# The Newton steps of the dilated heads' norms, on POOL instead of DVE, in a two-layer hybrid decoder trunk

## The chip, the cores and the metric

The kernel runs on one core of one Trainium2 chip. A core has five engines with a queue each: PE (TensorE, matrix products), DVE (VectorE) and ACT (ScalarE) for elementwise work, POOL (GpSimd), and SP, which only issues transfers here. Each engine works through its own row of instructions in order; where one needs what another engine makes, it waits on a semaphore and everything behind it in its row waits too. The metric is device time in microseconds (us) of one execution.

## The reference

Two layers over 256 tokens of width 1024. Each layer normalizes x, projects it by one wide matrix, and feeds three mixers: a causal convolution with 31 taps, a block-sparse attention with 8 heads ("NSA"), and three dilated banded attentions with 4 heads each. The change touches only the norm of the heads of the dilated queries and keys:

```python
def rms_norm(x, g):
    xf = x.astype(jnp.float32)
    y = xf * lax.rsqrt(jnp.mean(xf * xf, axis=-1, keepdims=True) + NORM_EPS)
    return (y * g.astype(jnp.float32)).astype(x.dtype)

def dilated_mixer(q, k, v, pos, qn, kn):
    ...
    for gi, (w, r) in enumerate(DIL_PAIRS):
        qh = rope(rms_norm(split_heads(qs[gi], DIL_HEADS), qn), pos)
        kh = rope(rms_norm(split_heads(kss[gi], DIL_HEADS), kn), pos)
        ...
        o, lse = banded_attention(phase(qh)[:, :, None], phase(kh), phase(vh), w // r, Q_BLOCK)
    ...

for l in range(DEPTH):
    h = rms_norm(x, attn_norm[l])
    (...) = jnp.split(h @ w_in[l], splits, axis=-1)
    x = x + jnp.concatenate([y_a, y_b, y_c], axis=-1) @ w_out[l]
    x = x + conv_ffn(rms_norm(x, ffn_norm[l]), w_up[l], ffn_dw[l], ffn_dw_b[l], w_down[l])
```

## The kernel before, in words

Tokens lie on the 128 partitions in two tiles. A product in full precision is made of three: the weights are split into `whi` (a rounded copy, made by ACT, line 210) and `wlo` (the rest, made by DVE, line 213), the activations in the same way, and PE adds three matmuls (lines 452 to 454). The weights stream in from memory in pieces of up to 128x1024 (`raw`); every piece passes ACT and DVE before PE can use it. `Dq`, `Dk`, `Dv` are the projections of the dilated queries, keys and values, `oa` and `ob` the output projection, `up` and `da`/`db` the feed-forward part.

`rope` (line 549 on) makes a normalized and rotated head tile. For each token tile DVE multiplies the projection by a cosine and a sine table into `z1` and `z2` and adds them; ACT squares the heads one at a time (line 568) and leaves the sums in `a` (`radq` or `radk`). Then the reciprocal root `r` of all heads at once (12 columns for the dilated heads) comes from a bit trick and three Newton steps: 12 small DVE instructions, each needing the one before it. At last DVE multiplies `z1` by `r` (`z1dq<-z1dq,rrdq`), PE transposes the result (`tpdq`, `tpdk`, line 880), and ACT copies it to `dq` or `dk`, from which the scores are made.

`dil_qk` calls `rope` four times in a layer: queries and keys (`dq`, `dk`), for each of two halves of the heads (0 and 1). With two layers that is eight chains of Newton steps. They stand in the mixer part of a layer, among the NSA pairs, the convolution's taps (`acc<-a_pad,dwh,acc`, 60 in a layer on DVE) and the splitting of weights. The string `ORDER` gives the order in which the program is written; a scheduler with a cost model of its own then sets each engine's row, so that an instruction that changes engine also moves others.

Of the kernel before, what the change touches and what calls it, by code (L numbers as in the profile page):

```python
# [14 lines left out]
I32 = mybir.dt.int32  # L15
AF = mybir.ActivationFunctionType
ALU = mybir.AluOpType
# [10 lines left out]
EPS = 1e-6  # L28
BIG = 1e30
TAPS = 31  # L30
MAGIC = float(0x5F3759DF)
# [157 lines left out]
def tile_hybrid_trunk(ctx, tc, x_in, pos_in, stream, feats, gains, norms, const_in, out):  # L189
    nc = tc.nc  # L190
# [21 lines left out]
    def tt(o, a, b, op):  # L212
        return nc.vector.tensor_tensor(out=o, in0=a, in1=b, op=op)  # L213

    def ts(o, a, s1, s2, op0, op1=None, eng=None):
        e = eng or nc.vector
        if op1 is None:
            e.tensor_scalar(out=o, in0=a, scalar1=s1, scalar2=None, op0=op0)
        else:
            e.tensor_scalar(out=o, in0=a, scalar1=s1, scalar2=s2, op0=op0, op1=op1)  # L220

    def stt(o, a, s, b, op0, op1):
        return nc.vector.scalar_tensor_tensor(out=o, in0=a, scalar=s, in1=b, op0=op0, op1=op1)  # L223
# [172 lines left out]
    def pool_tt(o, a, b, op):  # L396
        nc.gpsimd.tensor_tensor(out=o, in0=a, in1=b, op=op)
# [106 lines left out]
    for l in range(L):  # L504
# [45 lines left out]
        def rope(srcs, H, q, slots, nm, dup=False, np_=P):  # L550
            n = len(srcs)

            def small(tag):
                return mp.tile([P, n * H], F32, tag=tag, name=f"{tag}{nm}", bufs=2)[:np_]

            a, r, h_, t_ = (small(x) for x in ("ra", "rr", "rh", "rt"))
            z1s = []
            for i in range(n):
                v = srcs[i].rearrange("p (h d) -> p h d", h=H)
                z1 = mp.tile([P, H * 64], F32, tag="zr", name=f"z1{nm}{i}", bufs=ZB)[:np_].rearrange("p (h d) -> p h d", h=H)  # L560
                z2 = mp.tile([P, H, 64], F32, tag="z2", name=f"z2{nm}{i}", bufs=1)[:np_]
                cb = ctab[q][:np_, slots[i]].rearrange("p a b -> p (a b)").unsqueeze(1).broadcast_to([np_, H, 64])
                tt(z1, v, cb, ALU.mult)
                sb = stab[q][:np_, slots[i]].unsqueeze(1).broadcast_to([np_, H, 2, 32])
                tt(z2.rearrange("p h (a b) -> p h a b", a=2), v.rearrange("p h (a b) -> p h a b", a=2)[:, :, ::-1, :], sb, ALU.mult)
                sq = mp.tile([P, 64], F32, tag="sq", name=f"sq{nm}{i}", bufs=2)[:np_]
                for h in range(H):
                    nc.scalar.activation(out=sq, in_=v[:, h], func=AF.Square, accum_out=a[:, i * H + h:i * H + h + 1])  # L568
                tt(z1, z1, z2, ALU.add)
                z1s.append(z1)  # L570
            ts(a, a, 1.0 / 64.0, EPS, ALU.mult, ALU.add)
            ts(r.bitcast(I32), a.bitcast(I32), -0.5, MAGIC, ALU.mult, ALU.add)
            ts(h_, a, -0.5, None, ALU.mult)
            for _ in range(3):
                tt(t_, r, r, ALU.mult)
                tt(t_, t_, h_, ALU.mult)
                stt(r, t_, 1.5, r, ALU.add, ALU.mult)
            outs = []
            for i in range(n):
                rv = r[:, i * H:(i + 1) * H].unsqueeze(2)  # L580
                if dup:
                    d = mp.tile([P, H * 2 * 64], F32, tag="zr", name=f"zd{nm}{i}", bufs=ZB)[:np_]
                    tt(d.rearrange("p (h u d) -> p h u d", h=H, u=2), z1s[i].unsqueeze(2).broadcast_to([np_, H, 2, 64]),
                       rv.unsqueeze(3).broadcast_to([np_, H, 2, 64]), ALU.mult)
                    outs.append(d)
                else:
                    tt(z1s[i], z1s[i], rv.broadcast_to([np_, H, 64]), ALU.mult)
                    outs.append(z1s[i].rearrange("p h d -> p (h d)"))
            return outs
# [25 lines left out]
        def section_a(split):  # L615
            banks = tok_chunk("a", 512, split, f"A{l}")
            if split:
                late_loads()
            kss = []
            ksw = mp.tile([P, 3, 256], F32, tag="dk", name="ksw", bufs=1)  # L620
            for t in range(NT):
                bk = banks[t].rearrange("p (a e) -> p a e", a=2)
                ks = ksw[:, t]
                copy_act(ks.rearrange("p (a e) -> p a e", a=2), bk[:, :, 0:P])
                copy_act(vN[:, t], bk[:, :, P:2 * P])
                kss.append(ks)
            krs = rope(kss, 4, 1, (0, 1), "k", dup=True)
            for t in range(NT):
                kr = krs[t]
                tp = tp_bank(f"tpk{t}")  # L630
                for i in range(4):
                    nc.tensor.transpose(tp[:, i * P:(i + 1) * P], kr[:, i * P:(i + 1) * P], ident)
                tv = tp.rearrange("p (w g c) -> p w g c", w=2, g=2)
                split_keys(slice(P - t * P, 2 * P - t * P), tv[:, 0])
                split_keys(slice(272 + t * P, 272 + t * P + P), tv[:, 1])

        def section_a0(split):
# [43 lines left out]
            for g in range(2):  # L681
                nc.tensor.matmul(cp2[0:64, 64 + g * 64:128 + g * 64], hv[64:P, g].rearrange("p r c -> p (r c)"), w2[64:P], start=True, stop=True)
            kcd = rope([cp2[0:32, 0:64]], 1, 1, (2,), "c", dup=True, np_=32)[0]
            for g in range(2):
                tt(vbig[:, g], cp2[0:64, 64 + g * 64:128 + g * 64].unsqueeze(1).broadcast_to([64, 4, 64]),
# [13 lines left out]
        QS = mp.tile([P, 8, S], F32R, tag="QT", name="QS", bufs=1)  # L699
        banks = tok_chunk("b", 512, False, f"B{l}")  # L700
        qrs = rope(banks, 8, 0, (0, 1), "q")
        for t in range(NT):
            z = qrs[t].rearrange("p (h d) -> p h d", h=8)
# [167 lines left out]
        def dil_qk(nm, jp):  # L871
            q = 2 if nm == "q" else 3
            dst = mp.tile([P, 3, S], F32, tag=f"d{nm}", name=f"d{nm}{jp}", bufs=1)
            dil_state[nm] = dst
            banks = tok_chunk(f"d{nm}{jp}", 384, False, f"D{nm}{jp}{l}")
            zrs = rope([b[:, 0:384] for b in banks], 6, q, (0, 1), f"d{nm}{jp}")
            for t in range(NT):
                tp = tp_bank(f"tpd{nm}{jp}{t}")
                for i in range(3):
                    nc.tensor.transpose(tp[:, i * P:(i + 1) * P], zrs[t][:, i * P:(i + 1) * P], ident)  # L880
                copy_act(dst[:, :, t * P:(t + 1) * P], tp[:, 0:384].rearrange("p (k c) -> p k c", k=3))
# [80 lines left out]
        for step in ORDER.split():  # L962
            nm, arg = step[:-1].split("(")
            arg = int(arg) if arg.isdigit() else arg.split(",")
            if nm == "dq":
                dil_qk("q", arg)
            elif nm == "dk":
                dil_qk("k", arg)
            else:
                dict(np=nsa_pair, t=conv_taps, nf=nsa_finish, dv=dil_v, da=dil_attn, ds=dil_scores, pv=dil_pv, ct=lambda _: conv_tail())[nm](arg)  # L970

# [127 lines left out]
```

## Time and profile before

| | us |
|---|---|
| median of 3 runs | 751.72 (746.33 to 754.43) |
| the profiled execution, whole | 746.86 |
| its span, first to last instruction | 745.1 |
| PE busy in the span | 718.1 |
| DVE busy | 602.4 |
| ACT busy | 490.5 |
| POOL busy | 26.1 |

The span is 1.8 us shorter than the execution it belongs to. A share of busy time is a mean over stages. One layer takes from about 20 to 372 us, the other from there to the end; in each the mixers come first and the feed-forward part after them. Matmuls overlap in their records, so what PE really does per matmul is read from start to start. The same holds for DVE: its records overlap their neighbours by some 0.08 us.

### The profile page before, as it was taken

How to read it: one execution, taken by the hardware profiler on the slowest of the kernel's cores; microseconds unless marked ns; L12 is line 12 of the kernel's file. 1: busy time of each engine (PE TensorE's matmuls, PEld its weight loads, DVE VectorE, ACT ScalarE, POOL GpSimd, SP SyncE). 2: the span in 40 equal slices, each digit the busy share in tenths (PEclk: the TensorE clock that was granted, in tenths of full speed). 3: DMA queues.
4: the chain of work that ended last, by engine and by line, in shares of the span. 5: the costliest groups of instructions: out<-in, count | busy, mean ns of one | idle time of the engine just before them, and what ended most of it. 6: DMA issues, size and time to landing. Idle time of an engine off the chain costs nothing.

```text
span 745.1 us, 13477 instructions
## 1 busy us (share of the span) xinstructions
PE 718.1 (96%) x4818; PEld 635.4 (85%) x4818; DVE 602.4 (81%) x1393; ACT 490.5 (66%) x1174; POOL 26.1 (4%) x67
## 2 busy tenths in 40 slices
PE   6999989999999999999999998999999999999997
PEld 4789877887899999988877886779789999999885
DVE  7899999987898989944587699999878989988441
ACT  5867998756677667643356589986556767676330
POOL 6300000000000000000040000000000000000000
PEclk9999999999999999999999999999999999999999
DMA  8755123444466565665366231336344665666631
GB/s 312 254 154 149 46 72 114 142 166 160 132 224 209 180 205 185 197 206 196 115 225 211 78 109 40 93 86 187 111 142 170 203 200 193 200 197 197 198 115 56
DMA packets 36005, 119.77 MB, mean 161 GB/s; under 512 B 4113, under 2 KB 4385, under 8 KB 35938
## 3 DMA queue, kind: packets, MB, share of 16 engines
q1 hardware_dynamic: 35714, 118.63, 50.3%
q8 instruction: 38, 0.62, 0.3%
q0 software_dynamic: 224, 0.28, 0.2%
q14 instruction: 29, 0.24, 0.1%
HBM read 117.85 MB, written 1.05 MB: 160 GB/s over the span
## 4 chain that ended last, share of the span: by engine, by line
PE 80%; ACT 9%; DVE 7%; DMA 2%; issue 2%; POOL 0%; SPq 0%; DVEq 0%; ACTq 0%
PE up L454 10%; PE up L452 10%; PE up L453 10%; PE da L454 3%; PE da L452 3%; PE da L453 3%; PE db L452 3%; PE db L454 2%; PE db L453 2%; DVE wlo L213 2%; ACT whi L210 2%; ACT sqq L568 1%; PE o L827 1%; PE Dk L452 1%; PE Dk L453 1%
## 5 line engine op out<-in xcount | busy, mean ns | idle before, releaser
L213 DVE TENSOR_TENSOR wlo<-raw,whi 128x1024 fp32r<-128x1024 f32 (+3 forms) x232 | 259.4, 1125 | 79.8 <-ACT whi L210 79.1
L210 ACT ACTIVATE whi<-raw 128x1024 fp32r<-128x1024 f32 (+3 forms) x232 | 224.5, 980 | 97.6 <-PE db L454 53.6
L452 PE MATMUL up<-xT_hi,whi 128*128 128x256 f32 x640 | 176.8, 276 | 0.0
L453 PE MATMUL up<-xT_lo,whi 128*128 128x256 f32 x640 | 176.7, 276 | 0.0
L454 PE MATMUL up<-xT_hi,wlo 128*128 128x256 f32 x640 | 176.6, 276 | 0.0
L453 PEld LDWEIGHTS up<-xT_lo,whi 128*128 128x128 f32 x640 | 120.1, 188 | 0.0
L452 PEld LDWEIGHTS up<-xT_hi,whi 128*128 128x128 f32 x640 | 120.1, 188 | 0.0
L454 PEld LDWEIGHTS up<-xT_hi,wlo 128*128 128x128 f32 x640 | 120.1, 188 | 0.0
L223 DVE SCALAR_TENSOR_TENSOR u<-up,ffeat,u 128x255 f32<-128x255 f32 (+1 forms) x176 | 79.9, 477 | 2.6
L223 DVE SCALAR_TENSOR_TENSOR acc<-a_pad,dwh,acc 128x256 f32<-128x256 f32 x120 | 54.5, 477 | 0.2
L1052 ACT ACTIVATE sl<-u 128x256 f32<-128x256 f32 x44 | 18.1, 416 | 49.4 <-DVE u L223 49.4
L1045 ACT ACTIVATE u<-up,ffeat 128x256 f32<-128x256 f32 x88 | 44.2, 553 | 0.0
L453 PE MATMUL da<-wlo,gT_hi 128*128 128x512 f32 x88 | 34.3, 389 | 0.0
L452 PE MATMUL da<-whi,gT_hi 128*128 128x512 f32 x88 | 34.3, 389 | 0.0
L454 PE MATMUL db<-whi,gT_lo 128*128 128x512 f32 x88 | 34.2, 389 | 0.0
L454 PE MATMUL da<-whi,gT_lo 128*128 128x512 f32 x88 | 34.2, 389 | 0.0
L452 PE MATMUL db<-whi,gT_hi 128*128 128x512 f32 x88 | 34.2, 389 | 0.0
L453 PE MATMUL db<-wlo,gT_hi 128*128 128x512 f32 x88 | 34.2, 389 | 0.0
L452 PE MATMUL Dv<-whi,xT_hi 128*128 128x384 f32 x64 | 21.9, 347 | 2.7 <-ACT whi L210 2.0
L210 ACT ACTIVATE ms<-ms,dd 128x128 f32<-128x128 f32 (+1 forms) x64 | 24.3, 451 | 0.0
L452 PE MATMUL A<-whi,xT_hi 128*128 128x280 f32 (+1 forms) x64 | 22.9, 358 | 0.3 <-ACT xT_hi L210 0.2
L452 PE MATMUL Dq<-whi,xT_hi 128*128 128x384 f32 x64 | 22.7, 354 | 0.2
(358 smaller groups left out, 1601.4 us busy)
## 6 DMA issues: line engine op xcount, KB each, us to landing
raw<-in_stream SPq DMA_DIRECT2D x172, 512.0 KB, 4.2
raw<-in_stream SPq DMA_DIRECT2D x48, 384.0 KB, 3.3
raw<-in_stream SPq DMA_DIRECT2D x8, 280.0 KB, 4.7
w<-in_stream SPq DMA_DIRECT2D x4, 512.0 KB, 5.7
gain<-in_norms SPq DMA_DIRECT2D x3, 512.0 KB, 3.6
x<-in_x SPq DMA_DIRECT2D x4, 256.0 KB, 4.1
out<-x SPq DMA_DIRECT2D x4, 256.0 KB, 2.0
feat<-in_feats SPq DMA_DIRECT2D x2, 339.0 KB, 4.6
```

The lines of the kernel that those rows point to most:

```text
L210: return nc.scalar.activation(out=o, in_=i, func=AF.Copy, **kw)
L213: return nc.vector.tensor_tensor(out=o, in0=a, in1=b, op=op)
L223: return nc.vector.scalar_tensor_tensor(out=o, in0=a, scalar=s, in1=b, op0=op0, op1=op1)
L452: nc.tensor.matmul(o, a_hi, b_hi, start=start, stop=False)
L453: nc.tensor.matmul(o, a_hi, b_lo, start=False, stop=False)
L454: nc.tensor.matmul(o, a_lo, b_hi, start=False, stop=stop)
L568: nc.scalar.activation(out=sq, in_=v[:, h], func=AF.Square, accum_out=a[:, i * H + h:i * H + h + 1])
L827: nc.tensor.matmul(ob[j * 64:j * 64 + 64, 0:S], vv[0], pTs[pr][j][:, w, 0:2, :].rearrange("p a c -> p (a c)"), start=(w == 0), stop=False, ...
L1045: nc.scalar.activation(out=u[:, h], in_=z, func=AF.Identity, scale=c[:, 2:3], bias=c[:, 3:4])
L1052: nc.scalar.activation(out=sl_, in_=u[:, 0], func=AF.Silu)
```

## The change

For the chains whose name begins with "d" (dilated queries and keys) the Newton steps are issued to POOL. [...] The heads of the NSA mixer keep theirs on DVE.

```diff
-            ts(a, a, 1.0 / 64.0, EPS, ALU.mult, ALU.add)
-            ts(r.bitcast(I32), a.bitcast(I32), -0.5, MAGIC, ALU.mult, ALU.add)
-            ts(h_, a, -0.5, None, ALU.mult)
-            for _ in range(3):
-                tt(t_, r, r, ALU.mult)
-                tt(t_, t_, h_, ALU.mult)
-                stt(r, t_, 1.5, r, ALU.add, ALU.mult)
+            if nm[0] == "d":
+                pool = nc.gpsimd
+                ts(a, a, 1.0 / 64.0, EPS, ALU.mult, ALU.add, eng=pool)
+                ts(r.bitcast(I32), a.bitcast(I32), -0.5, MAGIC, ALU.mult, ALU.add, eng=pool)
+                ts(h_, a, -0.5, 1.0, ALU.mult, ALU.mult, eng=pool)
+                for _ in range(3):
+                    pool_tt(t_, r, r, ALU.mult)
+                    pool_tt(t_, t_, h_, ALU.mult)
+                    ts(t_, t_, 1.5, 1.0, ALU.add, ALU.mult, eng=pool)
+                    pool_tt(r, t_, r, ALU.mult)
+            else:
...
```

The scheduler also gives the rows of DVE, PE and ACT another order. SP's row of transfers stays as it was. Three places show it. The first is DVE at the first query chain (half 0, layer 1), from the row behind the tap that follows the last score reduction; `mn` and `cs` belong to the NSA mixer, `dd` and `ms` to its softmax. Before:

```order
L220 TENSOR_SCALAR radq_1020<-radq_1020 128x12
L806 TENSOR_REDUCE mn_1281<-cs_874 128x8
L220 TENSOR_SCALAR rrdq_1021<-radq_1020 128x12
L218 TENSOR_SCALAR rhdq_1022<-radq_1020 128x12
L213 TENSOR_TENSOR cs_874<-cs_874,mn_1281 128x128
L213 TENSOR_TENSOR rtdq_1023<-rrdq_1021 128x12
L223 SCALAR_TENSOR_TENSOR acc<-a_pad,dwh,acc 128x256
L213 TENSOR_TENSOR rtdq_1023<-rtdq_1023,rhdq_1022 128x12
```

and now, from the same row on:

```order
L817 TENSOR_REDUCE mn_1287<-cs_874 128x8
L223 SCALAR_TENSOR_TENSOR acc<-a_pad,dwh,acc 128x256
L213 TENSOR_TENSOR cs_874<-cs_874,mn_1287 128x128
L223 SCALAR_TENSOR_TENSOR acc<-a_pad,dwh,acc 128x256 x2
L213 TENSOR_TENSOR z1dq_1024<-z1dq_1024,rrdq_1021 128x384
L213 TENSOR_TENSOR z1dq_1036<-z1dq_1036,rrdq_1021 128x384
L792 RECIPROCAL dd_1082<-dd_1082 128x8
L765 ISA ms_1329,negm_1327<-sc_1332,cst 128x128
L765 ISA negm_1327 128x1
L213 TENSOR_TENSOR dd_1082<-dd_1082,sg 128x8
L213 TENSOR_TENSOR wlo_1193<-raw_1190,whi_1192 128x768
L213 TENSOR_TENSOR wlo_1211<-raw_1208,whi_1210 128x768
```

From there 27 rows stood ahead of the multiply by `r` before, both `wlo` pieces among them; now it is five instructions, and the two pieces stand behind it. The second place is POOL's row, where the chain stands alone (`pool_tt` is line 397; `rt` is the Newton scratch, `rh` minus half the mean square); it begins so and goes on with two more steps:

```order
L542 TENSOR_TENSOR stab_348<-sin_t,gsc_204 128x128
L220 TENSOR_SCALAR radq_1020<-radq_1020 128x12
L220 TENSOR_SCALAR rrdq_1021<-radq_1020 128x12
L220 TENSOR_SCALAR rhdq_1022<-radq_1020 128x12
L397 TENSOR_TENSOR rtdq_1023<-rrdq_1021 128x12
L397 TENSOR_TENSOR rtdq_1023<-rtdq_1023,rhdq_1022 128x12
L220 TENSOR_SCALAR rtdq_1023<-rtdq_1023 128x12
L397 TENSOR_TENSOR rrdq_1021<-rtdq_1023,rrdq_1021 128x12
```

Ahead of it stands only the making of the tables at the start of the layer, and nothing but the other chains behind it until the next layer's tables. The third place is PE at the second query chain (half 1, layer 1). Before:

```order
L454 MATMUL Dv_0_2035<-whi_1828,xT_lo 128x384
L452 MATMUL Dv_0_2035<-whi_1846,xT_hi 128x384
L880 MATMUL tpdq_1785<-ident,z1dq_1747 128x128 x3
L880 MATMUL tpdq_1790<-ident,z1dq_1759 128x128 x3
L453 MATMUL Dv_0_2035<-wlo_1847,xT_hi 128x384
```

and now:

```order
L454 MATMUL Dk_0_1815<-whi_1733,xT_lo 128x384
L452 MATMUL Dk_1_1816<-whi_1733,xT_hi 128x384
L891 MATMUL tpdq_1794<-ident,z1dq_1753 128x128 x3
L891 MATMUL tpdq_1799<-ident,z1dq_1765 128x128 x3
L453 MATMUL Dk_1_1816<-wlo_1734,xT_hi 128x384
```

The six transposes stood among the value projection's matmuls and now stand among the key projection's, ahead of the rest of it. Counted by the matmuls of lines 452 to 454 that stand ahead of them in PE's row, the transposes of the eight chains moved up from 354 to 338, 378 to 370, 487 to 463 and 547 to 528 in layer 1, and from 2248 to 2238, 2287 to 2268, 2371 to 2359 and 2434 to 2424 in layer 2: 118 matmuls in all, 19 of them (those of the second key chain of layer 1) the 512 wide ones of the output projection and the others 384 wide.

## Rows read from the trace of the kernel before

**Rows 1.** The page's first part: busy us, share of the span, instructions.

```profile
PE 718.1 (96%) x4818; PEld 635.4 (85%) x4818; DVE 602.4 (81%) x1393; ACT 490.5 (66%) x1174; POOL 26.1 (4%) x67
```

**Rows 2.** Busy us by stretch: PE, PEld, DVE, ACT, POOL; then clock, DMA share, GB/s.

```profile
60.00:190.00 130.00, 126.55 (x796) 105.69 (x796) 116.73 (x369) 98.91 (x311) 0.00 (x0) 1.00 0.37 118
205.00:372.00 167.00, 167.00 (x1212) 156.72 (x1211) 129.15 (x206) 100.94 (x152) 0.00 (x0) 1.00 0.61 191
440.00:570.00 130.00, 124.87 (x792) 103.19 (x791) 114.67 (x355) 98.32 (x303) 0.00 (x0) 1.00 0.34 106
```

**Rows 3.** The same from last square to multiply, eight chains: first, last, sum.

```profile
86.06:91.57 5.51, 5.03 (x37) 4.00 (x36) 5.39 (x27) 5.51 (x18) 0.00 (x0) 1.00 0.04 6
...
516.43:523.58 7.15, 7.15 (x39) 6.57 (x37) 6.70 (x18) 4.66 (x7) 0.00 (x0) 1.00 0.93 315
sum 44.66, PE 41.91 PEld 37.44 DVE 42.81 ACT 32.13 POOL 0.00; mean PE 5.24 PEld 4.68 DVE 5.35 ACT 4.02 POOL 0.00
```

**Rows 4.** Timeline of ACT: the last square of the first query chain.

```profile
85.86 0.20 ACT L568 ACTIVATION_READ_ACCUMULATOR sqdq<-Dq 128x1 f32 x1
```

**Rows 5.** Timeline of DVE, first query chain: start, duration, instruction.

```profile
86.24 0.17 DVE L220 TENSOR_SCALAR radq<-radq 128x12 f32<-128x12 f32 x1
86.32 0.28 DVE L806 TENSOR_REDUCE mn<-cs 128x8 f32<-128x128 f32 x1
...
86.94 0.48 DVE L223 SCALAR_TENSOR_TENSOR acc<-a_pad,dwh,acc 128x256 f32<-128x256 f32 x1
87.34 0.16 DVE L213 TENSOR_TENSOR rtdq<-rtdq,rhdq 128x12 f32<-128x12 f32 x1
...
91.57 1.02 DVE L213 TENSOR_TENSOR z1dq<-z1dq,rrdq 128x384 f32<-128x384 f32 x2
```

**Rows 6.** Timeline of PE: second query chain, then the output projection.

```profile
140.73 0.33 PE L453 MATMUL Dk<-wlo,xT_hi 128*128 128x384 f32 x1
140.91 0.33 PE L454 MATMUL Dk<-whi,xT_lo 128*128 128x384 f32 x1
...
144.92 0.99 PE L880 MATMUL tpdq<-ident,z1dq 128*128 128x128 f32 x6
...
158.04 0.39 PE L453 MATMUL oa<-wlo,yT_hi 128*128 128x512 f32 x1
158.27 0.39 PE L454 MATMUL oa<-whi,yT_lo 128*128 128x512 f32 x1
```

**Rows 7.** Timeline of POOL: a norm's root and Newton steps, one column.

```profile
8.91 0.26 POOL L220 TENSOR_SCALAR naa<-ssa 128x1 f32<-128x1 f32 x1 [4.17 <-ACT junk L335]
9.26 0.18 POOL L220 TENSOR_SCALAR naa<-naa 128x1 f32<-128x1 f32 x1
9.53 0.57 POOL L220 TENSOR_SCALAR nra<-naa 128x1 int32<-128x1 int32 x1
...
10.45 0.34 POOL L220 TENSOR_SCALAR nwta<-nra,nwha 128x1 f32<-128x1 f32 x1
10.90 0.27 POOL L220 TENSOR_SCALAR nra<-nwta,nra 128x1 f32<-128x1 f32 x1
...
13.30 2.81 POOL L220 TENSOR_SCALAR gsc<-grow 128x64 f32<-128x64 f32 x12
```

**Rows 8.** Timeline of DVE and POOL around 30 us: both with SBUF inputs.

```profile
27.15 1.22 DVE L213 TENSOR_TENSOR wlo<-raw,whi 128x1024 fp32r<-128x1024 f32 x1
29.67 0.59 POOL L542 TENSOR_TENSOR ctab<-cos_t,gsc 128x192 f32<-128x192 f32 x1
29.76 1.59 DVE L213 TENSOR_TENSOR wlo<-raw,whi 128x1024 fp32r<-128x1024 f32 x1 [1.39 <-ACT whi L210]
31.27 1.48 DVE L213 TENSOR_TENSOR wlo<-raw,whi 128x1024 fp32r<-128x1024 f32 x1
31.63 1.43 POOL L542 TENSOR_TENSOR ctab<-cos_t,gsc 128x128 f32<-128x128 f32 x1
33.03 0.45 POOL L542 TENSOR_TENSOR stab<-sin_t,gsc 128x128 f32<-128x128 f32 x1
```

More of the change, by code (lines that the diff above doesn't have):

```diff
@@ L570, in rope @@
                 z1s.append(z1)
-            ts(a, a, 1.0 / 64.0, EPS, ALU.mult, ALU.add)
-            ts(r.bitcast(I32), a.bitcast(I32), -0.5, MAGIC, ALU.mult, ALU.add)
-            ts(h_, a, -0.5, None, ALU.mult)
-            for _ in range(3):
-                tt(t_, r, r, ALU.mult)
-                tt(t_, t_, h_, ALU.mult)
-                stt(r, t_, 1.5, r, ALU.add, ALU.mult)
+            if nm[0] == "d":
[9 more added lines that the diff above has]
+            else:
+                ts(a, a, 1.0 / 64.0, EPS, ALU.mult, ALU.add)
+                ts(r.bitcast(I32), a.bitcast(I32), -0.5, MAGIC, ALU.mult, ALU.add)
+                ts(h_, a, -0.5, None, ALU.mult)
+                for _ in range(3):
+                    tt(t_, r, r, ALU.mult)
+                    tt(t_, t_, h_, ALU.mult)
+                    stt(r, t_, 1.5, r, ALU.add, ALU.mult)
             outs = []
```

## The prediction

> **What bounds the kernel now.** The first part of the page comes first: PE is busy for 718.1 of 745.1 us and DVE for 602.4, POOL for 26.1 [rows 1]. Those are means, so the next view is the busy time by stretch [rows 2]. In the feed-forward part PE is busy for all of 167.00 us. In the mixer parts PE is busy for 126.55 and 124.87 of 130 us and DVE for 116.73 and 114.67: PE idles 3.45 and 5.13 us there, DVE 13.3 and 15.3. The granted clock is 1.00 throughout, the upper of the two levels (2.4 GHz). The third view cuts out the eight stretches that the change is about, from the end of a chain's last square on ACT to the start of the multiply by `r` on DVE [rows 3]. The first runs from 86.06 us [rows 4] to 91.57 [rows 5]. Together they last 44.66 us, a mean of 5.58, and in them DVE is busy for 42.81 us and PE for 41.91. So in just these places both are full. The reader is to see that a chain of 12 small operations takes 5.58 us not because DVE is slow at it, but because other work stands between its steps: a step costs DVE 0.08 us from start to start (86.24 to 86.32), a tap 0.40 (86.94 to 87.34) [rows 5]. The chain is slow, and it costs next to nothing.
>
> **What DVE gets back.** Twelve instructions by 0.08 us are 0.96 us a chain, 7.7 us in eight chains. This is all that the change can give DVE, whose 28.6 us of idle time in the mixers say that not all of it would reach the end.
>
> **What the chain costs on POOL.** No row shows POOL at 128x12. The nearest one-input rows are a norm's steps at one column [rows 7]: from start to start 0.35 (8.91 to 9.26), 0.27 (9.26 to the next start at 9.53) and, with two scalars per partition, 0.45 us (10.45 to 10.90). All ten instructions of that norm took from 8.91 to 13.30, 0.44 each. The nearest two-input row is 0.45 us at 128 columns, with 0.59 at 192 [rows 8]: 0.0022 us a column, so about 0.19 at 12 columns, an estimate, plus the 0.09 that lie between the end of one dependent step and the start of the next (9.26 + 0.18 to 9.53) [rows 7]. That is 0.28. I take 0.35 a step, the middle of 0.27 to 0.45, since the steps are of both kinds and each depends on the last: 15 x 0.35 = 5.25 us. The bounds are 15 x 0.28 = 4.2 and 15 x 0.45 = 6.75.
>
> The Trainium skill ("GPSIMD Engine Reference", section 4.1) puts two-input elementwise work on POOL at about twice DVE's time and one-input work at about the same rate. By that rule, from the 0.16 us of such an operation on DVE [rows 5], nine two-input steps and six others would take 9 x 0.32 + 6 x 0.16 = 3.8 us in place of 5.25, and the whole change would cost some 12 us less than the sum below. The rows here have POOL at 0.27 to 0.45 us for a column, so I stay with them.
>
> **What the two engines cost each other.** Alone a `wlo` of 1024 columns takes 1.22 us; beside POOL's products two of them took 1.59 and 1.48, and a POOL product that takes 0.45 alone took 1.43 [rows 8]. So where DVE reads two inputs from SBUF, one waits for the other and they take turns: each turn costs DVE 0.26 to 0.37 us. Taps and `wlo` pieces are such instructions. I take four turns a chain, for the few DVE instructions that stand beside its start (next part), of 0.3 us: 1.2 us. The bounds are none and twice that.
>
> **Where the wait goes.** The multiply by `r` now waits for POOL, and in DVE's row it has moved up. At the first query chain a reduction, a subtraction and three taps lie between the last square and the multiply, 0.2 + 0.2 + 3 x 0.4 = 1.6 us. Read in the same way from the new row with the durations of before, the other seven have 1.6 to 2.5 us; the sum is 15.4, a mean of 1.9. The chain takes 5.25 + 1.2 = 6.45 us. DVE stands still or is slowed for 6.45 - 1.9 = 4.55 us a chain, gets 0.96 back, and loses 3.6. Eight times that is 29 us. Queued behind the multiply are the NSA softmax's reciprocal and reductions and two `wlo` pieces, for which the next `Dv` matmuls wait. ACT has the copies of the transposes ahead of its scaling of scores, and waits too. POOL's row holds nothing that anyone else waits for, and SP's transfers keep their order, so both cost nothing.
>
> PE gives a second count. Its transposes stand 118 matmuls further up, 99 by 0.18 us and 19 by 0.23 [rows 6]: 22.2 us of work that filled the wait before and now comes behind it. At the second query chain PE would stand at its transposes where it was at 140.73, and `r` comes no earlier than before, when they began at 144.92 [rows 6]. On top the result is later by 6.45 - 5.58 = 0.9 us a chain, 7 us in eight. That makes 29 us again. The two counts are one loss seen from two engines, not two losses.
>
> **The sum.** What can take some of it away is the idle time that PE already has in the mixers, 8.6 us at most; I take 5. So +24 us. Against the profiled execution (746.86 us, 1.8 us more than its span) that gives 771. The median of the three runs, 751.72, is 4.9 us above that execution; from it I get 775.7 and, as the later runs will lie between such levels, I forecast **774**. Low end: 4.2 us a chain and no turns, so 4.2 - 1.9 - 0.96 = 1.3, eight times 10.7, less 8.6: +2, or 754. High end: 6.75 + 2.4 = 9.15, less 1.9 and 0.96: 6.3, eight times 50, less 8.6: +42, or 794. From this I take 757 to 794.
>
> **Rivals.**
> *The wait is absorbed.* The scheduler's rows show where it believes `r` to be ready, and what stands ahead is not all: PE may fill its waits with other rows, and each chain's lateness may run into time that DVE (28.6 us) and PE (8.6) idle away already [rows 2]. With the low price of 1.3 us a chain this gives 751.72 + 2 = 754, within 1%. Against it stands that both engines are full in exactly the eight stretches [rows 3].
> *Faster.* If a step on POOL took 0.19 us and the next began at once, the chain would last 2.9 us; the wait, 1.0, is then paid by the 0.96 that DVE gets back, and the products, 2.7 us earlier than now, let PE keep its new order without a stall. That is the point from which it decides: 2.9 us. Below it DVE's 7.7 us could come through, and the time would be 744. For it speaks that DVE is full in the eight stretches [rows 3], so that relief counts there; against it that no dependent pair of POOL's steps is nearer than 0.27 us [rows 7].
> *The two engines take turns throughout.* If the last square ends while DVE still has a long stretch of taps ahead of the multiply, every step of POOL waits for a tap (0.40 us) and holds the next by 0.3: 15 x 0.70 = 10.5 us. Then `r` is 4.9 us later than now instead of 0.9, 32 us more in eight chains, and the time some 800. The Trainium skill ("SBUF — State Buffer", "Who interferes with whom") says that a DVE instruction with two SBUF inputs contends with a POOL instruction that reads SBUF; by that rule the turns are to be expected wherever taps run, and the rows around 30 us agree (1.59 against 1.22 us). It needs more DVE work beside the chain than the new rows show.
>
> **How the numbers follow.** Forecast 0.73, absorbed 0.13, turns throughout 0.09, faster 0.05. A measurement of this kernel tells about 1% from no change. The lower edge of the forecast lies under 759 with 0.04, and part of the fast case is within 1%: faster 0.04, same 0.16, slower 0.80. The range leaves out the faster case, most of the absorbed one and half of the turns.
>
> **What the profile would show.** POOL with 15 instructions a chain at 0.28 to 0.45 us where DVE waits, and longer beside taps; DVE idle for 3 to 4 us before `z1dq<-z1dq,rrdq` and `z1dk<-z1dk,rrdk`, with POOL as releaser; PE idle before `tpdq` and `tpdk`, released by DVE; the feed-forward part as long as before. If the multiply's wait is under 1 us a chain, the price of a step is wrong; if the waits are there and the time is not, it is the absorption.

## The result, and the profile after

The changed kernel takes 787.81 us (median of 4 runs, 782.06 to 794.5), the kernel before 750.69 beside it: a ratio of 1.048 with a 95% interval of 1.042 to 1.053. It is 37 us slower by the medians, and 36 by the ratio, which leaves out the slowest run (794.5), as that one was in a slower state. The forecast was 774, 24 us slower by its sum, in a range of 757 to 794: the direction, the waits and the range held, and 13 us were not foreseen. They have a cause of their own, which the prediction did not count at all: PE's clock.

The page's first part answers to [rows 1]; the clock's line is from its second part, one digit for each fortieth of the span.

```profile
PE 741.0 (94%) x4818; PEld 651.9 (83%) x4818; DVE 595.0 (75%) x1297; ACT 494.2 (63%) x1174; POOL 57.6 (7%) x187
```

```profile
PEclk9999989999999999999999999899999999999999
```

DVE got back what was reckoned: 602.4 - 595.0 = 7.4 us of busy time (forecast 7.7), and POOL took on 31.5. But PE is now busy for 741.0 us with the same 4818 matmuls, 23 more than before, and idle for 789.1 - 741.0 = 48.1 us of the span, where it was 745.1 - 718.1 = 27.0. So there are two losses, one of idle time and one of slower work. The stretches that answer to [rows 2] separate them (the mixers now begin and end later; columns as there):

```profile
60.00:190.00 130.00, 115.58 (x692) 95.55 (x690) 98.05 (x294) 90.34 (x295) 15.74 (x60) 0.93 0.29 95
225.00:392.00 167.00, 167.00 (x1192) 157.39 (x1191) 125.45 (x192) 98.74 (x149) 0.00 (x0) 1.00 0.61 190
456.00:586.00 130.00, 113.72 (x660) 91.88 (x660) 95.58 (x282) 90.98 (x296) 15.86 (x60) 0.93 0.29 90
```

In the feed-forward part PE stays full, at a clock of 1.00. In the same 130 us of a mixer PE is busy for 11 us less than before, did 104 and 132 matmuls fewer, and its granted clock is 0.93 where it was 1.00.

The eight stretches from last square to multiply answer to [rows 3]:

```profile
85.92:90.79 4.87, 3.05 (x26) 2.01 (x24) 1.86 (x6) 3.81 (x12) 3.68 (x15) 1.00 0.01 2
...
556.74:562.69 5.95, 2.98 (x18) 2.65 (x16) 2.21 (x3) 2.95 (x4) 4.76 (x15) 1.00 0.73 246
sum 41.11, PE 22.88 PEld 19.14 DVE 13.96 ACT 22.65 POOL 31.61; mean PE 2.86 PEld 2.39 DVE 1.74 ACT 2.83 POOL 3.95
```

The reader is to see two things. The chain on POOL is not slow: 41.11 / 8 = 5.14 us, 0.44 less than the 5.58 that it took on DVE, so `r` comes earlier than before. And the stretches have emptied: DVE is busy for 13.96 us of them in place of 42.81, PE for 22.88 in place of 41.91. Here is the first of them, first on POOL (start, duration, instruction):

```profile
86.33 0.51 POOL L220 TENSOR_SCALAR rrdq<-radq 128x12 int32<-128x12 int32 x1
...
87.08 0.37 POOL L397 TENSOR_TENSOR rtdq<-rrdq 128x12 f32<-128x12 f32 x1
...
88.22 0.21 POOL L397 TENSOR_TENSOR rrdq<-rtdq,rrdq 128x12 f32<-128x12 f32 x1
88.52 0.21 POOL L397 TENSOR_TENSOR rtdq<-rrdq 128x12 f32<-128x12 f32 x1
...
90.55 0.21 POOL L397 TENSOR_TENSOR rrdq<-rtdq,rrdq 128x12 f32<-128x12 f32 x1
```

then on DVE, whose two taps are the last work ahead of the multiply, as [rows 5] had its steps:

```profile
86.90 0.88 DVE L223 SCALAR_TENSOR_TENSOR acc<-a_pad,dwh,acc 128x256 f32<-128x256 f32 x2
90.79 1.03 DVE L213 TENSOR_TENSOR z1dq<-z1dq,rrdq 128x384 f32<-128x384 f32 x2 [3.01 <-POOL rrdq L397]
```

and on PE, where the transposes follow and then the value projection [rows 6]:

```profile
88.63 0.34 PE L453 MATMUL Dv<-wlo,xT_hi 128*128 128x384 f32 x1
91.41 1.14 PE L891 MATMUL tpdq<-ident,z1dq 128*128 128x128 f32 x6 [2.44 <-DVE z1dq L213]
...
92.98 0.52 PE L453 MATMUL Dv<-wlo,xT_hi 128*128 128x384 f32 x1
93.30 0.52 PE L454 MATMUL Dv<-whi,xT_lo 128*128 128x384 f32 x1
```

While DVE is at work POOL's first five steps take 0.20 to 0.51 us; from 87.94 on, when DVE stands still, 0.20 to 0.21, one each 0.29 us. DVE waits 3.01 us for `r`, PE 2.44 for the product. The last two lines are what the prediction lacks: after that wait the 384 wide matmuls start 0.32 us apart (92.98 to 93.30), and before the change 0.18 (140.73 to 140.91 [rows 6]). The stretches around it say why (the number after the five engines is the granted clock):

```profile
89.00:91.40 2.40, 0.00 (x0) 0.00 (x0) 0.61 (x2) 0.73 (x1) 1.26 (x7) 1.00 0.00 0
...
92.40:95.40 3.00, 3.00 (x12) 2.90 (x11) 3.00 (x7) 1.55 (x5) 0.00 (x0) 0.50 0.43 117
95.40:100.00 4.60, 4.21 (x28) 3.29 (x26) 2.97 (x14) 4.01 (x15) 0.00 (x0) 0.98 0.26 95
```

PE was idle for 2.4 us, took up work, and soon had the lower of the two levels (0.50: 1.2 GHz) for some 3 us, in which it did 12 matmuls and is called busy for all of it.

This happens behind each of the eight waits, and nowhere else while PE works. Eight windows laid around the work that follows them, 5 us at the queries and at the second keys, 10 us at the first keys, all have a mean clock of 0.66; the first two and their sum are

```profile
91.40:96.40 5.00, 4.99 (x23) 4.68 (x24) 5.00 (x19) 2.38 (x7) 0.00 (x0) 0.66 0.45 141
107.80:117.80 10.00, 9.38 (x45) 6.36 (x45) 8.25 (x29) 7.46 (x18) 0.00 (x0) 0.66 0.13 42
...
sum 50.00, PE 47.36 PEld 38.71 DVE 37.08 ACT 26.76 POOL 0.22; mean PE 5.92 PEld 4.84 DVE 4.63 ACT 3.35 POOL 0.03
```

and each stretch between them, from 20 to 788 us, has 1.00. So 50 x 0.34 = 17 us of PE's full speed are missing. The waits over the whole span (total us, times, longest), of PE

```profile
PE tpdk L891 <- DVE z1dk L213: 13.6, 4, 3.6
PE tpdq L891 <- DVE z1dq L213: 9.7, 4, 2.7
```

and of DVE:

```profile
DVE z1dk L213 <- POOL rrdk L397: 14.2, 4, 3.7
DVE z1dq L213 <- POOL rrdq L397: 11.7, 4, 3.3
```

There was none of these before. PE's come to 23.3 us (the eight last 2.3 to 3.6), DVE's to 25.9.

**A ledger.** A lower clock costs time that no view calls a wait. A span multiplied by one minus its mean granted clock is the time that PE would have saved at full speed, if PE is the bound: before 745.1 x 0.002 = 1.5 us, after 789.1 x 0.022 = 17.4. So the change adds 21.1 us of idle PE and 15.9 of slow PE, 37.0 together, against 44.0 between the two profiled executions and 37 between the medians. (Some 4 of the 7 that are over lie in the first feed-forward part of this one execution, 174.7 us in place of 170.4; the same 4 us appear in an experiment below that loses nothing, so they are not the change's.)

### The profile page after: what moved, and what is told of

Read it like the earlier page. It is cut to its first block, busy times and chain, and to the rows that moved or that the text cites. A ratio compares the mean times of both kernels' runs of the same rounds, so it can differ in the third digit from the quotient of the medians.

```text
span 789.1 us, 13513 instructions
## 1 busy us (share of the span) xinstructions
PE 741.0 (94%) x4818; PEld 651.9 (83%) x4818; DVE 595.0 (75%) x1297; ACT 494.2 (63%) x1174; POOL 57.6 (7%) x187
## 4 chain that ended last, share of the span: by engine, by line
PE 57%; issue 28%; DVE 7%; POOL 4%; ACT 2%; DMA 1%; SPq 0%; DVEq 0%; POOLq 0%; ACTq 0%
PE up L454 9%; PE up L453 9%; PE up L452 9%; PE da L453 3%; PE da L452 3%; PE da L454 3%; PE db L452 2%; PE db L453 2%; PE db L454 2%; DVE wlo L213 2%; ACT whi L210 1%; PE oa L454 1%; PE oa L452 1%; PE oa L453 1%; POOL rtdq L397 1%
## 5 line engine op out<-in xcount | busy, mean ns | idle before, releaser
L452 PE MATMUL Dv<-whi,xT_hi 128*128 128x384 f32 x64 | 24.0, 381 | 2.2 <-ACT sqdk L568 1.4
L453 PE MATMUL Dv<-wlo,xT_hi 128*128 128x384 f32 x64 | 24.2, 379 | 0.0
L454 PE MATMUL Dv<-whi,xT_lo 128*128 128x384 f32 x64 | 24.2, 383 | 0.0
```

The costliest lines, as they stand in the source:

```text
L452: nc.tensor.matmul(o, a_hi, b_hi, start=start, stop=False)
L453: nc.tensor.matmul(o, a_hi, b_lo, start=False, stop=False)
L454: nc.tensor.matmul(o, a_lo, b_hi, start=False, stop=stop)
```

## The experiments

Theory: POOL's chain is harmless, the waiting for it is not; the order of work puts the multiply and the transposes where `r` would be after some 2 us, and each wait is paid twice, as idle time and then in the clock. Rivals: DVE and POOL disturb each other at the memory; the new order is slow by itself. All times are against runs of the kernel before beside them. The ledger's two terms stand in each row as what they add to 27.0 and 1.5 us; "span" is what the profiled span adds to 745.1. Clock and ledger are those of the one profiled execution. The kernel before has 0.990 to 1.000 in its other executions and e11_fill_early 0.972 to 0.986, so a clock term is good to a few us; those of the change (0.977 to 0.982), e8_pin (0.977 to 0.980) and e4_warm (0.992 to 0.996) lie well apart in all their executions.

| kernel | us | ratio (95%) | clock | idle + | clock + | span + |
|---|---|---|---|---|---|---|
| the change | 787.8 | 1.048 (1.042 to 1.053) | 0.978 | 21.1 | 15.9 | 44.0 |
| e1_nowait | 749.3 | 1.001 (0.998 to 1.004) | 0.996 | -3.2 | 1.5 | 8.1 |
| e2_dead_pool | 756.0 | 1.011 (1.006 to 1.015) | 0.995 | 1.8 | 2.3 | 8.2 |
| e3_hold | 790.8 | 1.057 (1.052 to 1.061) | 0.981 | 30.0 | 13.5 | 42.6 |
| e4_warm | 775.9 | 1.038 (1.032 to 1.044) | 0.992 | 1.4 | 4.7 | 28.8 |
| e5_fill | 790.5 | 1.057 (1.053 to 1.060) | 0.985 | 29.5 | 10.3 | 42.6 |
| e6_hold3 | 778.3 | 1.040 (1.037 to 1.044) | 0.982 | 19.8 | 12.5 | 34.7 |
| e7_one_step | 757.3 | 1.014 (1.010 to 1.018) | 0.998 | 7.9 | 0.0 | 9.5 |
| e8_pin | 784.9 | 1.049 (1.046 to 1.052) | 0.978 | 18.7 | 15.7 | 37.1 |
| e9_fill_late | 770.4 | 1.027 (1.021 to 1.033) | 0.992 | 12.5 | 4.6 | 22.0 |
| e10_q_only | 764.3 | 1.019 (1.014 to 1.025) | 0.987 | 8.2 | 8.4 | 17.3 |
| e11_fill_early | 777.4 | 1.037 (1.031 to 1.044) | 0.972 | 16.3 | 20.4 | 35.8 |
| e12_three | 768.5 | 1.023 (1.016 to 1.031) | 0.983 | 6.8 | 11.5 | 20.0 |

But for e1_nowait (9.8 us over, 8 to 9 of it in its two feed-forward parts, 4 in each) and e4_warm, which gives PE some 20 us more to do, idle and clock together come to within 7 us of what the span adds. No row needs a third term of size.

**e1_nowait: POOL works, nobody waits.**

```diff
-                ts(a, a, 1.0 / 64.0, EPS, ALU.mult, ALU.add, eng=pool)
+                a2 = t_
+                ts(a2, a, 1.0 / 64.0, EPS, ALU.mult, ALU.add, eng=pool)
...
-                rv = r[:, i * H:(i + 1) * H].unsqueeze(2)
+                rv = (a if nm[0] == "d" else r)[:, i * H:(i + 1) * H].unsqueeze(2)
```

> POOL still does its 15 steps for every one of the eight head norms, but the DVE multiply takes the raw sums of squares from ACT, so nothing waits for POOL (left out: the head norms of the dilated queries and keys reach no output). Theory (PE and DVE wait for the POOL chain, and PE runs at half clock after such a wait): the 23.3 us of PE waits at tpdq and tpdk and the 25.9 us of DVE waits go, the granted clock is back near 1.0, and the time is 745 to 757 us, the 751 of before. Rival one (POOL and DVE disturb one another at the shared memory): POOL's steps still lie beside DVE work, so 8 to 20 us of the 37 stay: 760 to 772 us. Rival two (the other order of work that the change brings is slow by itself): the order of this kernel has the transposes earlier still, so the loss stays: 775 us or more.

749.27 us, before 748.66: the whole loss is gone, although POOL does its 120 steps beside a DVE that is full (its eight chains last 5.4 to 8.7 us there). Both rivals fall as an explanation of the 37 us: the disturbance, which would leave 8 to 20, and the order by itself, whose transposes stand earlier still here. It also shows what the change could have given at best: with DVE relieved and no wait at all the time is that of before, since PE is the bound (busy for 729.4 of 753.2 us there).

**e2_dead_pool: the same steps on POOL beside DVE's own.**

```diff
+            if nm[0] == "d":
+                pool = nc.gpsimd
+                a2, r2, h2, t2 = (mp.tile([P, n * H], F32, tag=x, name=f"{x}{nm}", bufs=1)[:np_] for x in ("pa", "pr", "ph", "pt"))
+                ts(a2, a, 1.0 / 64.0, EPS, ALU.mult, ALU.add, eng=pool)
...
             ts(a, a, 1.0 / 64.0, EPS, ALU.mult, ALU.add)
```

> The kernel before, with the chain on DVE as it was, and beside it the same 15 steps on POOL for each of the eight head norms, into tiles that nobody reads. It has before's waits and about before's order of work, and the POOL and DVE steps lie side by side. Theory: POOL's chain costs nothing if nobody waits for it: 748 to 757 us, at most 0.5 us a chain more (before 751). Rival (DVE and POOL disturb one another): in the chain on DVE its 12 steps of 0.08 us are held up by POOL's, 1 to 2 us a chain: 760 us or more.

756.02 us, 7.4 more than the runs of before beside it, 0.9 a chain: between the theory's bound (0.5 a chain) and the rival's 1 to 2. At the second key chain of layer 1 POOL's steps stand so:

```profile
153.70 1.03 POOL L220 TENSOR_SCALAR padk<-radk 128x12 f32<-128x12 f32 x1 [11.17 <-ACT sqdk L568]
...
155.09 1.05 POOL L220 TENSOR_SCALAR phdk<-padk 128x12 f32<-128x12 f32 x1
```

and DVE beside them:

```profile
153.44 1.22 DVE L213 TENSOR_TENSOR wlo<-raw,whi 128x1024 fp32r<-128x1024 f32 x1 [1.67 <-ACT whi L210]
...
154.84 1.24 DVE L213 TENSOR_TENSOR wlo<-raw,whi 128x1024 fp32r<-128x1024 f32 x1
```

POOL's step lasts until DVE's piece ends, and the piece takes what it takes alone (1.22 us [rows 8]). So POOL pays for the meeting and DVE does not: DVE's busy time is 603.4 us where it was 602.4. Half of the 7 us is in the ledger; which part of the rest is the meeting and which the slightly other order is open (the chains on DVE last 6.7 us there in place of 5.58, and the edit also gives the scratch tile of the squares one buffer in place of two).

**e3_hold and e6_hold3: the transposes put back.** Order edges hold PE's transposes behind a later matmul; e3_hold holds those of all four chains of a layer, e6_hold3 not those of the second keys.

```diff
+HOLD = {'q0': ('Dv0', 6), 'k0': ('Dv0', 14), 'q1': ('Dk1', 14), 'k1': ('out', 8)}
...
+        for key, (at, n) in HOLD.items():
+            if nm[:-1] == at and n == count[nm]:
+                for x in held[key + nm[-1]]:
+                    tc.add_manual_dep(x.ins, ins.ins.name, mybir.DependencyInfo(
+                        mybir.DependencyClass.NoSync, mybir.DependencyReason.DATA))
```

> The changed kernel, with the PE transposes of the eight normed tiles put back behind a fixed matmul of a later projection (behind matmul 18 or 42 of the next projections, or 24 of the output projection), which puts 6 to 52 matmuls more ahead of them, 154 in all, some 29 us at 0.19 us. POOL's chain, its 5.1 us and the DVE multiply that waits for it stay. Theory: PE's 23 us of waits at the transposes fall to under 8, and with them half of the half clock that follows: 757 to 772 us. Rival one (DVE and POOL disturb one another): nothing changes there, 780 us or more. Rival two (DVE's own 26 us of waits, which stay, are what delays the rest): 775 us or more.

790.76 us: nothing gained. PE's waits of e3_hold over the span:

```profile
PE Dv L454 <- DVE wlo L214: 9.3, 3, 3.2
PE tpxf L358 <- DVE xnf L224: 8.0, 3, 3.9
PE lnv L867 <- ACT acc L863: 6.5, 2, 3.2
...
PE tpdq L903 <- DVE z1dq L214: 2.8, 3, 1.3
```

The 23.3 us at the transposes are down to 2.8, and PE waits elsewhere: for `wlo`, which stands on DVE behind the waiting multiply, and at the end of the mixer (`lnv`, `tpxf`), since the second keys were held 16 us past their data. I had expected 757 to 772; the second rival's figure, 775 or more, came true. e6_hold3 takes that placing away:

> As e3_hold, but the transposes of the second pair's keys stay where the changed kernel has them, since in e3_hold they were held some 16 us past their data and what reads them was late. The waits for POOL on DVE stay at 26 us. If e3_hold lost by that placing alone: PE's waits at the transposes are 7 us (the two that are not held) of 23, and the time is 762 to 772 us. If DVE's waits for POOL delay as much as PE's did (the split of weights that queues behind the waiting multiply on DVE, and that the projections need): PE waits for wlo instead, and the time stays at 778 us or more.

778.33 us: the bad placing was worth 12 us, and what is left just reaches the rival's figure (778 or more; the runs lie at 776.1 to 781.6). PE's waits:

```profile
PE Dv L454 <- DVE wlo L214: 9.3, 3, 3.2
PE tpdk L903 <- DVE z1dk L214: 7.3, 2, 3.7
```

With 2.8 us at `tpdq` these come to 19.4 us, where the kernel adds 19.8 of idle time. A wait on DVE's queue reaches PE by whatever stands behind it there. Moving PE's own rows back gives little while DVE stands still (1.040 against 1.048, with intervals that overlap), and the clock stays at 0.982.

**e4_warm and e8_pin: PE kept at work.** In e4_warm three matmuls, whose result the transposes overwrite, stand ahead of each chain's transposes; both kernels pin the transposes behind a matmul near where the changed kernel has them, and e8_pin is the control without the three.

```diff
+                for _ in range(0 if t else 3):
+                    xs.append(nc.tensor.matmul(tp[0:12, 0:512], dil_state["h" + nm], dilm[:, 0:512], start=True, stop=True))
```

> The changed kernel, its transposes pinned where they were to within a few matmuls, with three matmuls of 128x12 by 128x512 put ahead of each chain's transposes, that read POOL's third result and are overwritten by the transposes: PE works some 2.5 us of each wait of about 3 instead of idling (some 33 matmuls fewer lie ahead in all, about 6 us). If a drop of the granted clock after each wait is a term of its own (10 to 15 us): the clock rises from 0.978 to 0.99 or more, and the time falls to 775 to 785 us although PE has 20 us more work. If the waits alone are the loss: the clock changes nothing, and the time is 788 to 798 us.

> The control for e4_warm: the same pins on the transposes, without the three matmuls ahead of them, which leaves the changed kernel's order but for a few matmuls. Each theory: 783 to 792 us, granted clock 0.975 to 0.985, PE's waits at the transposes 20 to 25 us. If it is under 780 us, e4_warm's gain came from the pins and not from a PE that is kept at work.

The control takes 784.87 us and e4_warm 775.85; by the ratios 0.0115 x 749 = 9 us less. Span and mean clock, of e4_warm

```profile
core 0: 773.9 us, clock 0.992
```

and of e8_pin:

```profile
core 0: 782.2 us, clock 0.978
```

PE has 24 matmuls more to do (48 records) and is done sooner. At the first query chain it fills the gap so:

```profile
89.84 2.74 PE L904 MATMUL tpdq<-cst,rhdq 128*12 128x512 f32 x6
92.52 0.87 PE L906 MATMUL tpdq<-ident,z1dq 128*128 128x128 f32 x6
```

(each of the three leaves two records) and the transposes follow without a wait. PE's waits at the transposes in e8_pin

```profile
PE tpdk L903 <- DVE z1dk L214: 13.3, 4, 3.6
PE tpdq L903 <- DVE z1dq L214: 8.7, 4, 2.7
```

come to 22.0 us, and in e4_warm

```profile
PE tpdk L906 <- DVE z1dk L214: 3.2, 4, 1.1
PE tpdq L906 <- DVE z1dq L214: 0.5, 1, 0.5
```

3.7 are left; the clock term falls from 15.7 to 4.7. The eight gaps are filled with some 22 us of work, and idle time falls by 17.3 us. Since the extra work takes the place of idling and gives nothing by itself, the gain is the clock's.

**e7_one_step: a shorter chain.**

```diff
-                for _ in range(3):
+                for _ in range(1):
                     pool_tt(t_, r, r, ALU.mult)
```

> The changed kernel with one of the three Newton steps (left out: the other two, so that the norms are less exact): 7 instructions on POOL in place of 15, a chain of some 2.8 us in place of 5.1. The program's order answers to the shorter chain and puts the transposes 64 matmuls earlier in all (12 us at 0.19 us). Theory (a wait is what the chain is longer than the order allows it): PE's waits at the transposes are 23 - 18 + 12 = 17 us, and the time is 772 to 784 us: two thirds of the loss stay although over half of POOL's steps are gone. Rival one (each POOL step costs by disturbing DVE): the loss shrinks with the steps, 7/15 of 37 us, 768 us or less.

757.25 us: my expectation, 772 to 784, was wrong, and the rival's figure (768 or less) nearer, for another reason than the rival's. The chain takes 2.4 us (the eight lie at 1.9 to 2.8) and the waits

```profile
PE tpdk L891 <- DVE z1dk L213: 5.1, 4, 1.6
PE tpdq L891 <- DVE z1dq L213: 4.9, 4, 1.7
```

are 10.0 us, none longer than 1.7: the shorter chain gives 8 x 2.75 = 22 us, which would leave 1.3, and 8.7 of them came back, where I had put 12 for the order's answer (in the trace the transposes stand 29 projection matmuls further up than in the changed kernel, some 5 us, and not 64; the rest is not shown). What I had not reckoned is that the clock term is then gone altogether: 0.998, as before the change. Of the 37 us the idle time gave 13 and the clock 16. Loss and steps are not in proportion: the waits of up to 1.7 us here cost themselves, those of 2.3 to 3.6 us in the changed kernel cost themselves and more than half as much again. The length of a wait alone does not decide it, though. In e3_hold a wait of 3.23 us for `wlo` (to 93.18 us) is followed by a clock of 1.00, and in e4_warm one of 1.65 us (to 95.05) by 0.50. The lines of the two:

```profile
93.10:100.00 6.90, 5.57 (x38) 4.99 (x39) 6.65 (x26) 6.58 (x35) 0.00 (x0) 1.00 0.37 114
```

```profile
96.60:99.90 3.30, 3.30 (x16) 3.13 (x14) 2.36 (x9) 2.54 (x16) 0.00 (x0) 0.50 0.13 51
```

What else decides it these runs do not show.

**e10_q_only: the queries alone.**

```diff
-            if nm[0] == "d":
+            if nm[:2] == "dq":
```

> The change made for the dilated queries alone; the keys' steps stay on DVE. Theory: a loss per wait, so the share of the queries' waits: 9.7 of the 23.3 us of PE's waits, and as much of the 37 us: 15 us, 762 to 770 us, with a granted clock of 0.985 to 0.992. If the loss comes from a queue that the waits of keys and queries fill up together, four chains alone cost far less: 757 us or less.

764.31 us, 15 us by the ratio, with 9.3 us of waits at the queries' transposes: as expected. The loss goes with the waits, but not one by one: of the 9.9 us that its clock takes in all, some 5 stand at two places that are not these waits (0.77 from 25 to 40 us, 0.57 from 104 to 108), and one of the four waits (2.3 us, to 470.6) has no drop behind it.

**e5_fill, e9_fill_late, e11_fill_early, e12_three: work beside the chain.** Convolution taps are put behind the z1 add (e5_fill) or behind POOL's third result (the others), and the multiply behind them:

```diff
+                seen = nc.vector.tensor_copy(mark, h_[:, 0:1])
...
+                with tc.issue_after(seen.ins):
+                    last = conv_taps(fill)
...
+                    with (tc.issue_after(last.ins) if fill else ExitStack()):
+                        tt(z1s[i], z1s[i], rv.broadcast_to([np_, H, 64]), ALU.mult)
```

> The changed kernel, but of the 60 convolution taps that DVE works through in each layer (0.477 us each) seven are placed between the last sum of each dilated query or key (z1 add) and its multiply, by order alone: 3.3 us of DVE work lie beside POOL's chain, where DVE now waits 3.2 us for it. Theory (the loss is that nothing lies beside POOL's chain): DVE's 25.9 us of waits for POOL fall to under 6, PE's 23.3 us at the transposes to under 8, the clock is at 0.99 or more, and the time is 750 to 765 us. Rival one (DVE and POOL disturb one another at the shared memory, the taps read two inputs there): POOL's steps grow from 0.29 us to 0.5 and the chain from 5.1 to 8 us, and the time stays at 770 us or more.

790.48 us, and DVE's waits are still 26.2. The edit missed its place. On DVE, at the second keys:

```profile
159.47 2.86 DVE L224 SCALAR_TENSOR_TENSOR acc<-a_pad,dwh,acc 128x256 f32<-128x256 f32 x7
166.32 1.03 DVE L214 TENSOR_TENSOR z1dk<-z1dk,rrdk 128x384 f32<-128x384 f32 x2 [3.99 <-POOL rrdk L398]
```

and on ACT the last square:

```profile
160.86 0.20 ACT L569 ACTIVATION_READ_ACCUMULATOR sqdk<-Dk 128x1 f32 x1
```

The taps begin 1.4 us before the last square, and at the other chains 2.7 to 8.5 us lie between the z1 add and that square. It says nothing of the theory.

> As e5_fill, whose seven taps DVE had done before the chain began, since ACT's last square comes 1.5 to 8.5 us after the z1 add that they were placed behind. Here nine taps (4.3 us) stand behind a copy of one element of POOL's third result, so that they can't run before POOL's chain is under way, and the multiply stands behind them. DVE is then busy beside POOL, as in e2_dead_pool, where POOL's chain of 15 took 4.5 to 7.9 us, 6.3 on average, in place of 5.0. Theory: DVE's 26 us of waits for POOL fall to under 10, PE's 23 us at the transposes to under 8 (the program's order puts the transposes behind more matmuls for the nine taps), the clock is at 0.99 or more, and the time is 750 to 765 us. Rival: POOL's chain, stretched by the taps to 8 us and more, ends later than now, the multiplies with it, and the time stays at 775 us or more.

770.38 us, 17 less than the change, 19 more than before. Here the taps stand where they should: DVE's waits are 4.9 us for POOL's last step and 7.6 for its third (under 10 together had been expected), PE's at the transposes 4.8, the clock is 0.992, these two as expected; the time is not (750 to 765). POOL beside taps

```profile
155.47 0.33 POOL L398 TENSOR_TENSOR rrdk<-rtdk,rrdk 128x12 f32<-128x12 f32 x1
155.87 0.31 POOL L398 TENSOR_TENSOR rtdk<-rrdk 128x12 f32<-128x12 f32 x1
```

needs 0.4 us a step, the chain 5.2 to 5.6, far from the rival's 8. On DVE

```profile
154.45 3.64 DVE L224 SCALAR_TENSOR_TENSOR acc<-a_pad,dwh,acc 128x256 f32<-128x256 f32 x9
158.78 1.03 DVE L214 TENSOR_TENSOR z1dk<-z1dk,rrdk 128x384 f32<-128x384 f32 x2 [0.69 <-POOL rrdk L398]
159.72 4.83 DVE L224 SCALAR_TENSOR_TENSOR acc<-a_pad,dwh,acc 128x256 f32<-128x256 f32 x12
```

a tap takes 0.40 us beside POOL as it did before [rows 5]. I took the late taps, done at 164.6 us, for what was left, and tried that:

```diff
-FILL = {("q", 0): 9, ("k", 0): 9, ("q", 1): 9, ("k", 1): 9}
+FILL = {("q", 0): 9, ("k", 0): 9, ("q", 1): 9, ("k", 1): 3}
```

The taps that stand between the chains are 30 here in place of 12.

> As e9_fill_late, where the taps were done 5.8 us after the last multiply of each layer (at 164.6 and 541.6 us, and in the changed kernel at 149.7 and 547.1, long before that multiply), and the mean over channels (lnm), which the convolution's end starts with, could only begin then. Here all taps but three are done before the last chain of a layer; nine stand beside each of the first three chains and three beside the last. If what e9_fill_late still loses (18.8 us) is the late end of the taps: 755 to 765 us. If it lies in what the taps delay on DVE behind every chain (weight splits, score minima): 766 us or more.

777.40 us: that explanation falls; the rest lies in what the taps delay on DVE, by the figure that was set for it, though which row is not shown. The clock is down to 0.972 in the profiled execution, the slowest, and at 0.979 to 0.986 in the others. e12_three gives the second keys back to DVE:

```diff
-            if nm[0] == "d":
+            if nm in ("dq0", "dk0", "dq1"):
```

> As e11_fill_early, and the last of the four chains of each layer (the second keys, whose scores come next) is on DVE as before, so that six chains of eight are on POOL with nine taps beside each, and no tap is late. Theory: no wait for POOL is left that nothing covers, the clock is above 0.99, and the time is 749 to 760 us; since PE is the bound and DVE's saved time is not on its path, not under 745 us. Rival: if DVE and POOL side by side cost 0.9 us a chain beyond that, as e2_dead_pool may say, 755 to 760 us.

768.54 us, above what either expected. The theory's 749 to 760 took for granted that waits go where they are covered; PE's waits at the transposes are 3.1 us here, and yet 6.8 us of idle time and 11.5 of clock are added, mostly in other places (the clock is 0.989 to 0.993 in the other three executions, of which two take 770 us, so that the split between the two terms does not hold for them). PE's longer waits tell where to look: in e9_fill_late 5.2 us at `tpxf` and 3.2 at `up`, at the end of the mixers (0.3 and 0.9 before), in e12_three 4.4 at `Dv` behind ACT's squares (0.4 before) and 2.5 at `tpcm`. None of the fills reaches the kernel before. Order edges on one engine of a full program move the waits.

## Why the prediction was right, and where it was off

**DVE's gain**, 7.7 us: 7.4 measured. By e1_nowait it is worth nothing to the end, as PE bounds.

**The price of a step on POOL**, 0.35 us (0.28 to 0.45): 0.29 with DVE still (88.22 to 88.52), 15 steps 4.4 us in place of 5.25. One input or two makes no difference at 12 columns (0.20 and 0.21). The nearest rows, one column wide, were the right kind of bound, and the low end was nearly the value. By the Trainium skill's rule ("GPSIMD Engine Reference", section 4.1; two inputs cost twice DVE's time, one input the same) the chain would be 3.8 us, an estimate; the trace has 5.14, and the ratio of the two kinds that the rule rests on is not there at this width.

**The turns**, 1.2 us a chain: 5.14 - 4.4 = 0.7. The term was mis-sized and half of it misplaced: a turn was to cost DVE 0.3 us, and it costs DVE nothing that the rows show (taps at 0.40, `wlo` at 1.22), while POOL's step is held until DVE's instruction is done (1.03 beside a `wlo`). The Trainium skill ("SBUF — State Buffer", "Who interferes with whom") says that the ports that the two share are held exclusively and that the order of issue decides who waits. The two rows of e2_dead_pool agree: `wlo` had begun 0.26 and 0.25 us before POOL's step.

**The wait on DVE**: the multiply was to stand still or be slowed for 4.55 us a chain; it waits 25.9 / 8 = 3.2, with 1.74 us of work in the stretch where 1.9 was reckoned. Of its price, 29 us net, 25.9 - 7.4 = 18.5 came.

**PE's count**: 22.2 us of work moved behind the transposes, plus 7 for a later `r`, less 5 for idle time that takes some in. The first stands. The second has the wrong sign: `r` comes 0.44 us a chain, 3.5 us in all, earlier. 22.2 - 3.5 = 18.7; measured are 23.3 us of waits there and 21.1 of added idle time. So +24 fits the idle time well, by errors that cancel. That 787.81 lies in the range is luck too: its upper end, 794, was made of dear steps (0.45 us) and twice the turns, and neither came; what brought the time up there is in no term.

**The step that failed is the sum**, which has no term for the clock. The prediction read a clock of 1.00 in [rows 2] and carried it over to a kernel in which PE would wait for 3 us eight times. Measured are 16 us more of it by the ledger; e4_warm shows the effect alone (9 us back by keeping PE at work), e7_one_step shows it absent where the waits at the transposes last 1.7 us at most, and in e1_nowait, which has none, it is 1.5 us. 24 + 16 is 40, and 37 were measured.

**The rivals.** Absorbed: no; e10_q_only shows the loss to follow the waits. Turns throughout (800): the taps do not hold POOL's steps long enough, 0.4 us each in e9_fill_late where 0.70 was feared. Faster: its point of decision, a chain of 2.9 us, was wrong, since e7_one_step has one of 2.4 us and is still 1.4% slower; a shorter chain also moves the transposes further up. Added up from the cases, the shares would have been 0.78 slower and 0.18 same, not 0.80 and 0.16; nothing hangs on it.

What stays open: which rows on DVE cost e9_fill_late, e11_fill_early and e12_three the rest, half of e2_dead_pool's 7 us, and why some waits of PE are followed by the lower clock and others of like length are not.

## What to carry to other kernels

Before taking a dependent chain off a full engine, ask what will stand beside it on its new one: the chain got no slower here (5.14 us in place of 5.58), and what it no longer overlapped with cost everything. If the order of work is set by costs, look in the order for how far the consumers have moved up, and price that in PE's matmuls. Then price each new wait of PE as idle time, and give the slower matmuls that may follow it a term of their own, from rows at the lower clock level: behind the eight waits of 2.3 to 3.6 us it came to two thirds of the waits again, behind those of up to 1.7 us in e7_one_step to nothing, and neither is a rule for another kernel. Read idle time and clock together: neither alone adds up to the span.

## What the hardware showed that was not expected

After PE's idle stretch of 2.4 us the granted clock did not fall at once: it is 1.00 in the stretch itself and 0.50 from about 0.8 us after the work begins again, for some 3 us, with matmuls 0.32 us apart in place of 0.18. The busy share hides this, for PE counts as busy throughout. In the same program the fall came 1.8 us after one wait (501.8 us) and 0.3 us before the end of another (170.7 us).

A step of 128x12 on POOL takes 0.20 us, is followed 0.29 us after its start by one that depends on it, and is stretched to 0.3 to 0.4 us beside DVE's taps and to 1.03 to 1.07 where a 128x1024 subtraction has just begun; DVE's instructions were not longer for it (1.22 to 1.23 and 0.47 to 0.49 us, as without POOL), unlike in [rows 8], where `wlo` took 1.48 and 1.59 us beside POOL products of 128 columns and more.
